# A 1024-wide mixer and attention program in float32 on one core: query, key and value products of 512 columns, a shared Nyquist row, gates behind the last pair, a later norm

## The chip, the core and the metric

The program runs on one core of one Trainium2 chip. The metric is device time in microseconds for one execution of the whole program. The profiled execution gives the span from the first to the last instruction and, for every instruction, its engine, start and duration.

## The reference, cut to what matters

512 tokens of width 1024 pass a feed-forward layer, a token mixer (short convolution, a recurrent part with eight heads of 64, two gates), a second feed-forward layer, a norm, a layer of Fourier mixing and attention ("even"), a recurrent layer ("odd") and a last norm. All is float32. The change touches the mixer's order and the even layer:

```python
def token_mixer(h, ...):
    p = h @ w_in
    pa, pb, pg = split(p)
    y_a = (b_gate * causal_dwconv(c_gate * u, conv_w)) @ w_out_a
    ...                                   # recurrent part of pb -> y
    y_b = (y * g) @ w_out_b
    g_a, g_b = split(pg)
    return (sigmoid(g_a) * y_a + sigmoid(g_b) * y_b) @ w_o

def fourier_attention_layer(x, norm_g, w_in, fourier_w, q_gain, k_gain, w_out, rope):
    h = rms_norm(x, norm_g)
    f_in, f_gate, q, k, v, a_gate = split(h @ w_in)      # 1024 1024 1024 256 256 1024
    fg = f_in.reshape(b, s, 4, 256)
    fmix = fftn(fg, axes=(1, 3), norm="ortho").real      # over tokens and 256 channels
    fmix = einsum('bsgc,gce->bsge', fmix, fourier_w)
    f_out = fmix * silu(f_gate)
    q = rope(rms_norm(q.reshape(b, s, 8, 128), q_gain))
    k = rope(rms_norm(k.reshape(b, s, 2, 128), k_gain))
    a_out = softmax(q k^T * 128 ** -0.5) v * silu(a_gate)   # four query heads to a key head
    return x + concat(f_out, a_out) @ w_out
```

## The kernel before

**Products.** Each float32 operand is split into a high part `h`, rounded to the matmul type, and a low part `l`; a product is three matmuls, h*h, h*l and l*h (`mm3`, L784). Activations lie feature-major: eight tiles of 128 features by 512 tokens, `xs` after the norm's gains. `gemm` (L790) makes 128 output features by 512 tokens: 8 k tiles x 3 = 24 matmuls of 512 columns, weights stationary. Query, key and value are wanted token-major, so `gemm_tm` (L1605) has the tokens stationary and the weights moving: for each of four token tiles 8 x 3 matmuls of 256 columns, six times over (four query groups of two heads, key, value).

**Weights.** `wload` (L739) fetches 512 KB into `raw` (three buffers), casts it into `wh` and subtracts into `wl` (four buffers each). In the first and second feed-forward layers `put_low` prepares and stores low parts of the mixer's and the odd layer's weights; `wload_low` (L756) fetches them in place of the subtraction. `group_tm` (L779) loads a group's weights in two pieces of four k tiles. Activations have 76 slots of 2 KB per partition, PSUM eight banks.

**Order.** `Rec` records every operation of the program and `schedule` (L317) plays it through with a table of costs: on each engine it issues the ready operation with the lowest `prio`, that is its place in the program plus `bias`, up to 800 places ahead of the first one not issued, as far as buffers are free. TensorE stays in its shape of matmul for some places (`choose`, L540). The order found is fixed in the program: each engine works it off in sequence. So moving a call in the program moves its priority. All instructions are recorded at one line, L555; the groups are told apart by their tiles.

**Mixer** (`_mixer`, L927). `pair(j)` prepares two heads (three products with `w_in`, chunk matrices, a small inverse through DRAM), `pair_out` (L1110) runs their recurrence in some fifty small steps and ends in `yo`, split into `ys`. `conv` and `out_a` with their gates, and the gates 34 to 41 (`gates`), are products of 24 matmuls that can lie beside these steps. `w_out_b` contracts over the four `ys`; its results, times the gates `gb` and plus `ga`, are `ms`, over which `w_o` contracts.

**Even layer** (`_even`, L1363). Two sums of squares give `rstd1` (the final norm) and `rstd` (with the layer's own norm, `rs` in the trace): adds on VectorE for the first, on GpSimd for the second, a sum over partitions by TensorE (`fold`, the tiles `rones`). For each of four groups of 256 channels: two products `e_f`, scaled by `rstd`; a transform over channels (`d1`); sum and difference of the token halves, `sd`; transforms over tokens (`seq`): `pc` of the first 128 columns, `pq` and `pn` of the second 128. Of `pn` only row 0, the Nyquist channel, is used. Then two gate products and the contraction with `fw`. After that `e_out0`, key and value, and for each query group `rot` (sum of squares, rotation), a factor of 1/rms, and two heads: gate product `e_ag`, transposes `to_fm`, scores, softmax, transposes of `e`, product with the values.

Of the kernel before, what the change touches and what calls it, by code (L numbers as in the profile page):

```python
# [142 lines left out]
def layout(i):  # L143
    f = lambda n: np.asarray(i[n], dtype=np.float32)
    o = {}
# [19 lines left out]
    o["e_qkv"] = _groups(np.ascontiguousarray(ei[:, 2048:3584]), 8, 256).reshape(6, 128, 2, 4, 256)  # L165
# [482 lines left out]
class Net:  # L648
# [130 lines left out]
    def group_tm(self, g):  # L779

        return [self.wload(self.a["e_qkv"][g][:, i], (128, 4, 256)) for i in range(2)]
# [145 lines left out]
    def _mixer(self):  # L927
# [84 lines left out]
        self.pair_out(*p.pop(0))  # L1012
        conv(3)
        p[3] = pair(3)
        out_a(0)
        self.pair_out(*p.pop(1))
# [4 lines left out]
        gates(0, 4)  # L1021
        self.pair_out(*p.pop(3))
        gates(4, 8)
# [339 lines left out]
    def _even(self):  # L1363
# [6 lines left out]
        xs = [self.split_scaled(x[k], g12[:, k:k + 1]) for k in range(KT)]  # L1370
        s1 = self.sumsq(adds="vector")
# [8 lines left out]
        V.tensor_tensor(rstd, rstd, rstd1, ALU.mult)  # L1380

# [30 lines left out]
        fo = []  # L1412
        for g in range(4):
# [23 lines left out]

            def seq(col, tr):
                ps = self.P((128, 2, 256))
                for e in range(2):  # L1440
                    h, l = sd[e]
                    for k in range(2):
                        self.mm3(ps[:, e], h[:, k, col], l[:, k, col], d2h[tr][e][:, k], d2l[tr][e][:, k], k == 0, k == 1)
# [7 lines left out]
            pn = seq(c2, 0)  # L1451
            V.tensor_copy(Q[0:1], pn[0:1])
# [42 lines left out]
        def tables(q):  # L1495
# [3 lines left out]
            for tp in range(2):  # L1499
                t = self.T(shape=(128, 2, 2, 128), p="rope")  # L1500
                for h in range(2):
                    G.tensor_tensor(t[:, :, h], rp[1][:, 2 * tp:2 * tp + 2],
                                    sw[:, q].unsqueeze(1).to_broadcast([128, 2, 128]), ALU.mult)
                s.append(t)
            return c, s

        def rot(g, tab):


            w = self.group_tm(g)  # L1510
            ms = self.sm(8)
            out = []
            for tp in range(2):
                ps = self.P((128, 2, 2, 128))
                for tt in range(2):
                    self.gemm_tm(ps[:, tt].rearrange("p h i -> p (h i)"), w, xs, 2 * tp + tt)
                s = self.T(shape=(128, 4, 128))
                A.activation(s, ps.rearrange("p t h i -> p (t h) i"), AF.Square)
                V.tensor_reduce(ms[:, 4 * tp:4 * tp + 4], s, axis=AX.X, op=ALU.add)
                t2 = self.T(shape=(128, 2, 2, 128))  # L1520
# [331 lines left out]
```

## Time and profile before

| | |
|---|---|
| median of 3 runs | 1857.87 us (1857.47 to 1860.03) |
| profiled execution | 1858.05 us, span 1856.3 us, mean granted clock 0.997 |
| TensorE, its weight loads | busy 1835.8 us (99%), 1540.4 us (83%) |
| VectorE, ScalarE, GpSimd | 1266.8 (68%), 854.5 (46%), 230.5 us (12%) |
| DMA | 341.10 MB, mean 184 GB/s |

A matmul's shown duration (0.39 us for 512 columns) is longer than the step from one to the next, because they are pipelined; the pace is read from starts or from a count over a stretch. TensorE's busy share therefore says where it waits, not how fast it is. The granted clock is in tenths of 2.4 GHz; 0.5 is its other level, 1.2 GHz. By the timeline the first feed-forward layer lies at 8 to 390 us, the mixer to about 780, the second feed-forward layer to 1140, the even layer to 1537, the odd layer to the end.

### The profile page before, as it was taken

What the parts mean: (1) busy time and instruction counts of PE and PEld (TensorE: products, weight loads), DVE (VectorE), ACT (ScalarE), POOL (GpSimd) and SP (SyncE); (2) the same over time, 40 slices, a digit from 0 to 9 for tenths busy, and PEclk for the clock granted to TensorE, in tenths of its full rate; (3) what the DMA queues carried; (4) which work ended last, traced back from release to release, by engine and by line L of the source; (5) the groups of instructions that cost most, each with busy time, mean ns of one, the idle gap of its engine ahead of it and who ended that gap; (6) DMA issues with size and microseconds to landing.
All of it is one profiled execution on the core that took longest, in us unless ns stands there. A gap on an engine that the chain in (4) does not pass through costs nothing.

```text
span 1856.3 us, 26407 instructions
## 1 busy us (share of the span) xinstructions
PE 1835.8 (99%) x10344; PEld 1540.4 (83%) x10344; DVE 1266.8 (68%) x1966; ACT 854.5 (46%) x1188; POOL 230.5 (12%) x182
## 2 busy tenths in 40 slices
PE   9999999999999999999999999999999999999997
PEld 7888888888888886888878887888999888888887
DVE  7766775579767424476567668854478966899773
ACT  6333433465243332344344246422255645897771
POOL 0100101223202003211011015110000010000002
PEclk9999999999999999999999999999999999999999
DMA  7898895436534344578888874222212125466543
GB/s 270 285 311 283 299 318 173 142 128 172 189 120 139 131 154 157 176 260 291 271 273 306 283 239 146 81 69 79 89 50 72 54 102 188 169 204 210 193 170 103
DMA packets 120398, 341.10 MB, mean 184 GB/s; under 512 B 33873, under 2 KB 36177, under 8 KB 120273
## 3 DMA queue, kind: packets, MB, share of 16 engines
q1 hardware_dynamic: 120272, 339.41, 54.6%
q8 instruction: 81, 1.33, 0.3%
q14 instruction: 45, 0.36, 0.1%
HBM read 277.76 MB, written 61.60 MB: 183 GB/s over the span
## 4 chain that ended last, share of the span: by engine, by line
PE 53%; DMA 6%; DVE 5%; ACT 1%; issue 1%; POOL 1%; SPq 0%; POOLq 0%; DVEq 0%; ACTq 0%
PE pm L555 51%; DMA raw<-o_in 3%; PE pw L555 2%; DVE wl L555 2%; DMA low<-wl 2%; ACT wh L555 1%; DMA raw<-ffn_d 1%; DVE t L555 0%; DVE l L555 0%; DMA wl<-low 0%; POOL acc L555 0%; DVE x L555 0%; DVE xl L555 0%; DVE acc L555 0%; DVE s L555 0%
## 5 line engine op out<-in xcount | busy, mean ns | idle before, releaser
L555 ACT CAST wh<-raw 128x1024 fp32r<-128x1024 f32 (+1 forms) x331 | 343.8, 1042 | 670.6 <-PE pm L555 285.2
L555 PE MATMUL pm<-xh,wl 128*128 128x512 f32 x1488 | 580.6, 390 | 1.3 <-DVE wl L555 1.1
L555 PE MATMUL pm<-xh,wh 128*128 128x512 f32 x1488 | 581.3, 391 | 0.3 <-ACT wh L555 0.3
L555 PE MATMUL pm<-xl,wh 128*128 128x512 f32 x1488 | 580.6, 390 | 0.9 <-DVE xl L555 0.9
L555 DVE TENSOR_TENSOR wl<-raw,wh 128x1024 fp32r<-128x1024 f32 (+1 forms) x302 | 383.1, 1271 | 194.9 <-DMA low<-wl 86.7
L555 PEld LDWEIGHTS pm<-xh,wl 128*128 128x128 f32 x1488 | 279.4, 188 | 60.9 <-DVE wl L555 3.9
L555 PEld LDWEIGHTS pm<-xh,wh 128*128 128x128 f32 x1488 | 279.4, 188 | 58.7 <-ACT wh L555 0.7
L555 PEld LDWEIGHTS pm<-xl,wh 128*128 128x128 f32 x1488 | 279.4, 188 | 58.6 <-DVE xl L555 1.3
L555 PE MATMUL pm<-h,wl 128*128 128x512 f32 (+1 forms) x832 | 317.8, 382 | 2.1 <-DMA wl<-low 2.1
L555 PE MATMUL pm<-h,wh 128*128 128x512 f32 (+1 forms) x832 | 316.8, 383 | 1.8 <-DVE yo L555 0.9
L555 PE MATMUL pm<-l,wh 128*128 128x512 f32 (+1 forms) x832 | 317.5, 382 | 0.0
L555 POOL TENSOR_TENSOR t<-t,t 128x512 f32<-128x512 f32 x60 | 90.3, 1507 | 915.3 <-DVE t L555 693.7
L555 PEld LDWEIGHTS pm<-h,wl 128*128 128x128 f32 x832 | 156.8, 189 | 32.3 <-DMA wl<-low 2.6
L555 PEld LDWEIGHTS pm<-h,wh 128*128 128x128 f32 x832 | 156.8, 189 | 32.4 <-DVE h L555 1.3
L555 PEld LDWEIGHTS pm<-l,wh 128*128 128x128 f32 x832 | 156.9, 189 | 30.1 <-DVE l L555 0.2
L555 DVE TENSOR_TENSOR t<-pm,rstd 128x512 f32<-128x512 f32 x146 | 98.8, 684 | 15.4 <-PE pm L555 15.3
L555 ACT ACT_TABLE_LOAD x72 | 92.4, 1283 | 17.2 <-DVE s L555 15.5
L555 DVE CAST wh<-raw 128x1024 fp32r<-128x1024 f32 x77 | 56.6, 735 | 63.9 <-PE pm L555 38.8
L555 DVE TENSOR_TENSOR x<-x,pm 128x512 f32<-128x512 f32 (+1 forms) x44 | 27.8, 637 | 68.7 <-PE pm L555 68.6
L555 ACT ACTIVATE t<-t 128x512 f32<-128x512 f32 x100 | 59.4, 625 | 26.7 <-DVE t L555 25.7
L555 POOL TENSOR_TENSOR acc<-acc,sq 128x512 f32<-128x512 f32 x28 | 46.7, 1667 | 151.1 <-ACT sq L555 151.1
L555 DVE TENSOR_TENSOR l<-t,h 128x512 fp32r<-128x512 f32 x87 | 59.7, 695 | 6.8 <-ACT h L555 5.7
(257 smaller groups left out, 2052.9 us busy)
## 6 DMA issues: line engine op xcount, KB each, us to landing
low<-wl SPq DMA_DIRECT2D x106, 512.0 KB, 3.7
wl<-low SPq DMA_DIRECT2D x106, 512.0 KB, 3.5
raw<-w_in SPq DMA_DIRECT2D x76, 512.0 KB, 4.7
raw<-o_in SPq DMA_DIRECT2D x64, 512.0 KB, 4.6
raw<-ffn_g SPq DMA_DIRECT2D x44, 512.0 KB, 4.2
raw<-ffn_u SPq DMA_DIRECT2D x44, 512.0 KB, 4.9
raw<-ffn_d SPq DMA_DIRECT2D x32, 512.0 KB, 4.9
raw<-o_out SPq DMA_DIRECT2D x32, 512.0 KB, 4.7
```

The source lines that it names most:

```text
L555: o.ins = getattr(getattr(self.nc, o.eng), o.fn)(*o.args, **o.kw)
```

## The change

Four things change. (1) The query, key and value weights are laid out as three groups of 512 columns (heads 0 to 3, heads 4 to 7, key with value), each loaded in four pieces of two k tiles; `gemm_tm` makes 512 columns for each token tile. `rot` works on one token tile, `factor` makes 1/rms for a whole group, and the loop runs over two groups of four heads. (2) Column 128 of every group's `sd` is copied into column 32 g of one zeroed tile pair `nyq`; one transform of it gives all four Nyquist rows in `pn`, so the Fourier part runs all four first halves, then this transform, then four second halves. (3) In the mixer `pair(3)` comes before `conv(3)`, the second pair's `pair_out` before `out_a(0)`, and all eight gates come behind the last `pair_out`. (4) The even layer's two sums of squares and factors are recorded with a `bias` of 100.

```diff
--- before.py
+++ after.py
@@ -162,7 +162,7 @@
     o["w_o"] = _groups(f("w_o")[0], 8, 128)
     ei = f("even_w_in_2")[0]
     o["e_f"] = _groups(np.ascontiguousarray(ei[:, 0:2048]), 8, 128)
-    o["e_qkv"] = _groups(np.ascontiguousarray(ei[:, 2048:3584]), 8, 256).reshape(6, 128, 2, 4, 256)
+    o["e_qkv"] = _groups(np.ascontiguousarray(ei[:, 2048:3584]), 8, 512).reshape(3, 128, 4, 2, 512)
     o["e_ag"] = _groups(np.ascontiguousarray(ei[:, 3584:4608]), 8, 128)
     fw = f("fourier_w_2")[0]
     lowr = fw[:, 0:128]
@@ -778,7 +778,7 @@
     def group_tm(self, g):
-        return [self.wload(self.a["e_qkv"][g][:, i], (128, 4, 256)) for i in range(2)]
+        return [self.wload(self.a["e_qkv"][g][:, i], (128, 2, 512)) for i in range(4)]
     def mm3(self, out, wh, wl, xh, xl, start, stop):
@@ -1010,17 +1010,16 @@
         conv(1)
         conv(2)
         self.pair_out(*p.pop(0))
+        p[3] = pair(3)
         conv(3)
-        p[3] = pair(3)
+        self.pair_out(*p.pop(1))
         out_a(0)
-        self.pair_out(*p.pop(1))
         out_a(1)
         out_a(2)
         self.pair_out(*p.pop(2))
         out_a(3)
-        gates(0, 4)
         self.pair_out(*p.pop(3))
-        gates(4, 8)
+        gates(0, 8)
         ms = []
         for h in range(4):
             w = self.group("w_out_b", h)
@@ -1368,6 +1367,8 @@
         o1, o2 = _VOFF["final_norm"], _VOFF["even_norm_2"]
         V.tensor_tensor(g12, self.vec[:, o1:o1 + 8], self.vec[:, o2:o2 + 8], ALU.mult)
         xs = [self.split_scaled(x[k], g12[:, k:k + 1]) for k in range(KT)]
+        self.rec.bias = 100
         s1 = self.sumsq(adds="vector")
         rstd1 = self.T(p="rs1")
         self.rsqrt(rstd1, s1, 1.0 / D, 1e-6)
@@ -1378,6 +1379,7 @@
         V.tensor_tensor(v2, v2, s2, ALU.mult)
         self.rsqrt(rstd, v2, 1.0 / D, 1e-6)
         V.tensor_tensor(rstd, rstd, rstd1, ALU.mult)
+        self.rec.bias = 0
         pt = self.W((128, 4, 128))
         for t in range(4):
@@ -1409,7 +1411,12 @@
             V.tensor_copy(p[0:1], fwr[0:1, 0, gs])
             V.tensor_copy(m[0:1], fwr[0:1, 1, gs])
             fw.append((p, m))
-        fo = []
+        nyq = [self.T(F32R, (128, 2, 2, 128), "ny") for _ in range(2)]
+        for t in nyq:
+            G.memset(t.bitcast(F32), 0.0)
+        sds = []
         for g in range(4):
             fs = []
             for m in range(2):
@@ -1434,11 +1441,22 @@
             V.tensor_tensor(s, pp[0], b, ALU.add)
             V.tensor_tensor(d, pp[0], b, ALU.subtract)
             sd = (self.split(s, (128, 2, 256)), self.split(d, (128, 2, 256)))
+            for e in range(2):
+                for t, hl in zip(nyq, sd[e]):
+                    nc.copy(t[:, e, :, 32 * g:32 * g + 1], hl[:, :, 128:129])
+            sds.append(sd)
+        ps = self.P((128, 2, 256))
+        for e in range(2):
+            for k in range(2):
+                self.mm3(ps[:, e], nyq[0][:, e, k], nyq[1][:, e, k], d2h[0][e][:, k], d2l[0][e][:, k], k == 0, k == 1)
+        pn = self.T(shape=(128, 2, 256), p="pn")
+        A.copy(pn, ps)
+        fo = []
+        for g in range(4):
             def seq(col, tr):
                 ps = self.P((128, 2, 256))
                 for e in range(2):
-                    h, l = sd[e]
+                    h, l = sds[g][e]
                     for k in range(2):
                         self.mm3(ps[:, e], h[:, k, col], l[:, k, col], d2h[tr][e][:, k], d2l[tr][e][:, k], k == 0, k == 1)
                 return ps
@@ -1448,8 +1466,7 @@
             pq = seq(c2, 1)
             Q = self.T(shape=(128, 2, 256))
             A.copy(Q, pq)
-            pn = seq(c2, 0)
-            V.tensor_copy(Q[0:1], pn[0:1])
+            V.tensor_copy(Q[0:1], pn[32 * g:32 * g + 1])
             Qs = self.split(Q, (128, 2, 256))
             fl = lambda t: t.rearrange("p e j -> p (e j)")
             if g % 2 == 0:
@@ -1492,78 +1509,87 @@
             nc.sync.dma_start(out=r, in_=self.a["rope"][:, i])
             rp.append(r)
-        def tables(q):
+        def tables(q, n):
             c = self.T(shape=(128, 4, 128), p="rope")
             G.tensor_tensor(c, rp[0], qkg[:, q].unsqueeze(1).to_broadcast([128, 4, 128]), ALU.mult)
             s = []
...
+            for t in range(4):
+                if t % (4 // n) == 0:
+                    r = self.T(shape=(128, 4, 128), p="rope")
+                o = n * (t % (4 // n))
+                G.tensor_tensor(r[:, o:o + n], rp[1][:, t:t + 1].to_broadcast([128, n, 128]),
+                                sw[:, q].unsqueeze(1).to_broadcast([128, n, 128]), ALU.mult)
+                s.append(r[:, o:o + n])
             return c, s
-        def rot(g, tab):
...
+        def rot(ps, t, n, tab, ms):
+            s = self.T(shape=(128, 4, 128))[:, 0:n]
+            A.activation(s, ps, AF.Square)
+            V.tensor_reduce(ms, s, axis=AX.X, op=ALU.add)
+            t2 = self.T(shape=(128, 4, 128))[:, 0:n]
+            half = lambda z: z.rearrange("p h (a b i) -> p (h a) b i", a=2, b=2)
+            V.tensor_tensor(half(t2), half(ps)[:, :, ::-1, :], half(tab[1][t]), ALU.mult)
+            V.tensor_tensor(s, ps, tab[0][:, t:t + 1].to_broadcast([128, n, 128]), ALU.mult)
+            G.tensor_tensor(s, s, t2, ALU.add)
+            return s
+        def factor(ms, n):
+            w = 4 * n
+            c = self.sm(16)[:, 0:w]
+            r, r2 = (z.rearrange("p (t h) -> p t h", h=2)[:, :, 0:1].to_broadcast([128, 4, n]) for z in (rt, rt2))
+            f = lambda z: z.rearrange("p (t h) -> p t h", t=4)
+            V.tensor_tensor(f(ms), f(ms), r2, ALU.mult)
             V.tensor_scalar(ms, ms, 1.0 / 128, 1e-6, op0=ALU.mult, op1=ALU.add)
...
-            V.tensor_tensor(c, c, rt, ALU.mult)
-            return out, c
+            V.tensor_tensor(f(c), f(c), r, ALU.mult)
+            return c
         def to_fm(tiles, h):
             ps = self.W((128, 4, 128))
             for t in range(4):
-                PE.transpose(ps[:, t], tiles[t // 2][:, 2 * (t % 2) + h], self.ident)
+                PE.transpose(ps[:, t], tiles[t][:, h], self.ident)
             return self.split(ps.rearrange("p t i -> p (t i)"))
...
+        w = self.group_tm(2)
+        ktab = tables(1, 2)
+        ms = self.sm(16)[:, 0:8]
+        kt, vT = [], []
+        for t in range(4):
+            ps = self.P((128, 4, 128))
+            self.gemm_tm(ps.rearrange("p h i -> p (h i)"), w, xs, t)
+            kt.append(rot(ps[:, 0:2], t, 2, ktab, ms[:, 2 * t:2 * t + 2]))
+            if t % 2 == 0:
+                vt = self.T(shape=(128, 2, 256))
+            V.tensor_scalar(vt[:, t % 2], ps[:, 2:4].rearrange("p h i -> p (h i)"), rt[:, 2 * t:2 * t + 1], None, op0=ALU.mult)
+            if t % 2:
+                vT.append(self.split(vt, (128, 2, 256)))
+        ck = factor(ms, 2)
+        for t in range(4):
+            V.tensor_tensor(kt[t], kt[t], ck[:, 2 * t:2 * t + 2].unsqueeze(2).to_broadcast([128, 2, 128]), ALU.mult)
         kF = [to_fm(kt, h) for h in range(2)]
...
-        qtab = tables(0)
+        qtab = tables(0, 4)
         at = []
-        for g in range(4):
-            qt, cq = rot(g, qtab)
+        for g in range(2):
+            w = self.group_tm(g)
+            ms = self.sm(16)
+            qt = []
+            for t in range(4):
+                ps = self.P((128, 4, 128))
+                self.gemm_tm(ps.rearrange("p h i -> p (h i)"), w, xs, t)
+                qt.append(rot(ps, t, 4, qtab, ms[:, 4 * t:4 * t + 4]))
+            cq = factor(ms, 4)
             V.tensor_scalar(cq, cq, 128.0 ** -0.5, None, op0=ALU.mult)
-            for hh in range(2):
-                h = 2 * g + hh
+            for hh in range(4):
+                h = 4 * g + hh
...
                         mx = self.sm(2, tag="mx")
                         V.tensor_reduce(mx[:, 0:1], sc, axis=AX.X, op=ALU.max)
-                        cc = cq[:, 2 * t + hh:2 * t + hh + 1]
+                        cc = cq[:, 4 * t + hh:4 * t + hh + 1]
                         V.tensor_scalar(mx[:, 0:1], mx[:, 0:1], cc, -1.0, op0=ALU.mult, op1=ALU.mult)
                         e = self.T(shape=(128, 4, 128), p="e")
                         A.activation(e.rearrange("p a i -> p (a i)"), sc, AF.Exp, bias=mx[:, 0:1], scale=cc,
@@ -1607,8 +1633,8 @@
         sl = slice(t * 128, t * 128 + 128)
         n = len(xs)
         for k, (xh, xl) in enumerate(xs):
-            h, l = w[k // 4]
-            self.mm3(out, xh[:, sl], xl[:, sl], h[:, k % 4], l[:, k % 4], k == 0, k == n - 1)
+            h, l = w[k // 2]
+            self.mm3(out, xh[:, sl], xl[:, sl], h[:, k % 2], l[:, k % 2], k == 0, k == n - 1)
     def odd(self):
```

## Rows read from the trace of the kernel before

**Rows 1.** The page, parts 1 and 2: busy time by engine; granted clock in 40 slices.

```profile
PE 1835.8 (99%) x10344; PEld 1540.4 (83%) x10344; DVE 1266.8 (68%) x1966; ACT 854.5 (46%) x1188; POOL 230.5 (12%) x182
...
PEclk9999999999999999999999999999999999999999
```

**Rows 2.** The chain of waits, a long run of 512-column products (start us, us, what).

```profile
955.21 162.35 PE pm L555 x715
```

**Rows 3.** The timeline of TensorE in the key product (start us, us, what).

```profile
1320.00 0.28 PE L555 MATMUL pm<-wh,xh 128*128 128x256 f32 x1
...
1321.20 0.28 PE L555 MATMUL pm<-wl,xh 128*128 128x256 f32 x1
```

**Rows 4.** Groups by form, whole span: busy us, mean ns of one, idle before.

```profile
L555 ACT CAST wh<-raw 128x1024 fp32r<-128x1024 f32 x315 | 330.3, 1052 | 637.4 <-PE pm L555 259.7 <-DMA raw<-ffn_u 74.1 <-DMA raw<-w_in 66.7
...
L555 PE MATMUL pm<-wh,xh 128*128 128x256 f32 x192 | 55.3, 288 | 0.0
```

**Rows 5.** Windows, us; TensorE, its loads, VectorE, ScalarE, GpSimd busy (count); clock, DMA, GB/s.

```profile
721.00:740.00 19.00, 15.09 (x59) 11.42 (x58) 13.55 (x17) 7.94 (x11) 14.65 (x10) 0.91 0.59 214
735.90:739.30 3.40, 3.40 (x8) 2.72 (x9) 3.05 (x3) 2.08 (x4) 3.40 (x3) 0.51 1.02 413
1140.00:1172.00 32.00, 28.83 (x124) 22.61 (x123) 27.79 (x30) 16.03 (x21) 9.48 (x3) 1.00 0.45 143
1172.00:1318.00 146.00, 146.00 (x768) 125.88 (x767) 86.11 (x123) 41.22 (x54) 10.44 (x10) 1.00 0.23 75
1395.10:1433.20 38.10, 38.10 (x257) 35.00 (x256) 32.28 (x74) 23.70 (x40) 2.56 (x3) 1.00 0.17 57
1433.20:1471.50 38.30, 38.30 (x257) 35.05 (x256) 35.39 (x92) 21.96 (x37) 2.59 (x3) 1.00 0.16 55
1471.50:1500.00 28.50, 28.08 (x161) 24.02 (x160) 24.62 (x68) 17.23 (x30) 0.16 (x1) 1.00 0.13 46
```

**Rows 6.** The chain of waits from 700 to 760 us.

```profile
721.41 0.82 DVE yo L555
...
728.88 6.96 DMA wl<-low
```

**Rows 7.** The timeline: one row of ScalarE, two of TensorE, one of VectorE.

```profile
671.09 0.58 ACT L555 COPY vT<-pw 128x512 f32<-128x512 f32 x1
...
1146.23 0.50 PE L555 MATMUL pm<-xl,wh 128*128 128x512 f32 x1 [0.91 <-DVE xl L555]
...
1150.41 0.50 PE L555 MATMUL pm<-h,rones 128*128 128x512 f32 x1 [2.19 <-ACT h L555]
...
1171.35 0.69 DVE L555 TENSOR_TENSOR rs<-rs,rs 128x512 f32<-128x512 f32 x1
```

**Rows 8.** The tile acc, 1110 to 1155 us: shortest/median/longest ns, first and last start.

```profile
L555 POOL TENSOR_TENSOR acc<-acc,sq x7: 1282/1742/5378, 1118.3 to 1144.3; 128x512 f32<-128x512 f32 x7
```

**Rows 9.** Groups by form from 670 to 721 us.

```profile
L555 PE MATMUL pm<-xh,wl 128*128 128x512 f32 x33 | 13.1, 397 | 0.0
...
L555 PE MATMUL pm<-h,wl 128*128 128x512 f32 x21 | 8.3, 395 | 0.0
```

**Rows 10.** Groups by form of VectorE from 1395.1 to 1433.2 us.

```profile
L555 DVE TENSOR_TENSOR wl<-raw,wh 128x1024 fp32r<-128x1024 f32 x4 | 4.9, 1216 | 0.6 <-ACT wh L555 0.6
...
L555 DVE TENSOR_TENSOR t<-pm,rope 128x512 f32<-128x512 f32 x4 | 2.8, 689 | 0.1
```

**Rows 11.** Groups by form from 1172 to 1318 us.

```profile
L555 ACT COPY t<-pm 128x512 f32<-128x512 f32 x8 | 4.7, 588 | 10.9 <-PE pm L555 10.8
...
L555 DVE COPY rt<-pw 128x8 f32<-128x8 f32 x1 | 0.2, 158 | 0.0
```

**Rows 12.** DMA issues, 1300 to 1500 us: count, KB each, median us to landing.

```profile
raw<-e_qkv SPq DMA_DIRECT2D x9, 512.0 KB, 3.6
```

**Rows 13.** The timeline of TensorE: last wide product, first narrow one behind it.

```profile
701.51 0.39 PE L555 MATMUL pm<-xl,wh 128*128 128x512 f32 x1
701.83 0.27 PE L555 MATMUL pw<-zb,MN 64*64 64x64 f32 x2
```

More of the change, by code (lines that the diff above doesn't have):

```diff
@@ L1498, in tables @@
             s = []
[L1499 to L1504, printed above, removed]
-            return c, s
-        def rot(g, tab):
[L1510 to L1520, printed above, removed]
-                V.tensor_tensor(t2.rearrange("p t h (a b i) -> p (t h a) b i", a=2, b=2),
-                                ps.rearrange("p t h (a b i) -> p (t h a) b i", a=2, b=2)[:, :, ::-1, :],
-                                tab[1][tp].rearrange("p t h (a b i) -> p (t h a) b i", a=2, b=2), ALU.mult)
-                V.tensor_tensor(s.rearrange("p (t h) i -> p t h i", t=2), ps,
-                                tab[0][:, 2 * tp:2 * tp + 2].unsqueeze(2).to_broadcast([128, 2, 2, 128]), ALU.mult)
-                G.tensor_tensor(s, s, t2.rearrange("p t h i -> p (t h) i"), ALU.add)
-                out.append(s)
-            c = self.sm(8)
-            V.tensor_tensor(ms, ms, rt2, ALU.mult)
@@ L1532, in rot @@
             V.reciprocal(c, c)
-            t = self.sm(8)
+            t = self.sm(16)[:, 0:w]
             V.tensor_tensor(t, c, c, ALU.mult)
@@ L1543, in to_fm @@
             for t in range(4):
-                PE.transpose(ps[:, t], tiles[t // 2][:, 2 * (t % 2) + h], self.ident)
+                PE.transpose(ps[:, t], tiles[t][:, h], self.ident)
             return self.split(ps.rearrange("p t i -> p (t i)"))
-        kt, ck = rot(4, tables(1))
-        for tp in range(2):
-            V.tensor_tensor(kt[tp], kt[tp], ck[:, 4 * tp:4 * tp + 4].unsqueeze(2).to_broadcast([128, 4, 128]), ALU.mult)
-        kF = [to_fm(kt, h) for h in range(2)]
-        w = self.group_tm(5)
@@ L1552, in _even @@
-        vT = []
-        for tp in range(2):
-            ps = self.P((128, 2, 256))
-            for tt in range(2):
-                self.gemm_tm(ps[:, tt], w, xs, 2 * tp + tt)
-            t = self.T(shape=(128, 2, 256))
-            V.tensor_tensor(t, ps, rt.rearrange("p (t h) -> p t h", h=2)[:, 2 * tp:2 * tp + 2, 0:1].to_broadcast([128, 2, 256]), ALU.mult)
-            vT.append(self.split(t, (128, 2, 256)))
-        qtab = tables(0)
-        at = []
-        for g in range(4):
-            qt, cq = rot(g, qtab)
+        w = self.group_tm(2)
```

## The prediction

> **What bounds the kernel now.** The page comes first: TensorE is busy 99% of the 1856.3 us span, its clock is at its upper level in every slice [rows 1]. So a gain must come from fewer or cheaper matmuls, or from the few places where TensorE waits or its clock falls. The pace is next. In a stretch without a wait, 715 matmuls take 162.35 us, 0.227 us for one of 512 columns [rows 2]; ten steps of 256 columns take 1.20 us, 0.120 us each [rows 3]. Two of 256 therefore cost 0.240 us against 0.227 for one of 512. The groups by form give the count for query, key and value: 192 of each of three kinds [rows 4]. The windows and TensorE's own waits give the places. From 721 to 740 us TensorE is idle 19.00 - 15.09 = 3.91 us [rows 5], behind the last pair's `yo` and a low part of `w_o`'s weights that takes 6.96 us to land [rows 6]. From 1140 to 1172 us 124 matmuls take 32.00 us where 124 x 0.227 = 28.15 would do: 3.85 us too long [rows 5]; the waits are for `xl` and for the sum of squares [rows 7].
>
> **The change part by part.** The sum is made against the profiled execution: span 1856.3 us, 1858.05 us with what lies around it, 0.18 us above the median.
>
> *Query, key and value.* 576 products of 256 columns become 288 of 512: 576 x 0.120 = 69.1 against 288 x 0.227 = 65.4 us. TensorE sets the pace there, so 3.7 us come off the path. Loads, splits of weights and elements read from PSUM stay; three factor chains in place of five and some narrower vector instructions are hidden beside TensorE. Two things may eat the gain. The weights of a group now fill all four `wh` and `wl` buffers; I cost this at nothing, because the first pair of k tiles is free once all four token tiles have used it, and a new one needs 1.05 us of cast and 1.22 us of subtraction [rows 4, 10], while the 18 products that follow on the last token tile take 4.1 us. The other is the order: the query products came in four blocks of 11.5 us between the heads and now come in two of 21.8. A cycle of two heads takes 38.10 us of TensorE and 32.28 of VectorE [rows 5]. Of the latter some 8.0 belong to the query block (two subtractions, four rotations at 0.69 [rows 10], reductions and factor, estimated from these), so a head without query products is 13.3 us on TensorE and 12.1 on VectorE, 91%. VectorE was at 35.39 of 38.30 and, without query products, 24.62 of 28.50 us in the last two stretches [rows 5]. At the first share the last four heads lose nothing; at the second they take 48.4 / 0.864 = 56.0 in place of 53.2 us. So this part is worth 0.9 to 4.1 us (3.7 and the 0.42 us of idle time in 1471.5 to 1500 [rows 5]); I take 3.7, since the first is the busier row.
>
> What is left beside the columns is 2 x 0.120 - 0.227 = 0.013 us a matmul [rows 2, 3]. [...]
>
> *Nyquist row.* Per group the third transform of the second stage (2 x 2 x 3 = 12 products) goes; one run of 12 does all four groups. 36 products fewer, 36 x 0.120 = 4.3 us. Added are two clears on GpSimd, 16 copies of one column (the copy of eight columns takes 0.16 us [rows 11]), one evacuation, and the last group's spectrum must be there before the first group's second half. VectorE is busy 86 of 146 us there [rows 5], and the first transforms of four groups, with products of the next group ready, cover each other. Without that cover it is one chain, once: an evacuation of 0.59 us [rows 11] and a row's copy, taken as long. I take 4.3, bounds 3.1 and 4.3.
>
> *Mixer.* The same products in another order of priority. The window says why TensorE ran dry: from 670 to 721 us, beside the last pair's chain, it did 98 products of gates (33 of two kinds, 32 of the third) and 63 of `w_out_b` (21 of each kind) [rows 9]; these ran out, and all that remained of `w_out_b` needed the last pair's result. Its weights still filled the buffers, so those of `w_o` came in one burst, one of them in 6.96 us [rows 6]. Behind it the clock was at 0.51 (1.2 GHz, the lower level) for 3.4 us, in which eight matmuls were started [rows 5], each 0.2 us longer: 1.6 us. With 3.91 idle this is 5.5 us. With the gates behind the last pair, its chain starts some four gates (4 x 24 x 0.227 = 21.8 us) earlier, and eight gates and three quarters of `w_out_b`, 43.6 + 16.3 = 59.9 us, lie beside a chain that took some 50 (its transposed values are copied at 671.09, `yo` begins at 721.41 [rows 6, 7]): `yo` should be there before the cover ends, and `w_o`'s weights come at the normal rate. What is late next is the sum of the last output column (multiply, GpSimd add, split), under 21 ready products of 4.8 us. I take 5.0, bounds 3.5 and 5.5. The fourth pair's start before the last convolution, and the second pair's end before the first `out_a`, only move cover from one chain to another. A change between wide and narrow products costs about 0.1 us (a step of 0.32 in place of 0.227 [rows 13]); some 20 such changes more or fewer make 2 us either way, taken as nothing.
>
> *Even layer's norm.* Its squares, adds and folds now stand 100 places later in priority. VectorE's seven adds no longer come ahead of `xl` and of the second weights; the folds, which stopped TensorE while GpSimd's last add took 5.38 us [rows 8], fall behind one or two more groups of `e_f`. The factor was ready at 1172 [rows 7]. If it slips by two groups (10.9 us) to 1183, `e_f` still has room: eight PSUM banks at 24 x 0.227 = 5.45 us each last from 1140 to 1183.6. Of 3.85 us I take 3.2; the low bound is 1.8 (the `xl` wait of 0.91 and half of the 2.19 us [rows 7] stay).
>
> Sum: 3.7 + 4.3 + 5.0 + 3.2 = 16.2 us, 1858.05 - 16.2 = 1841.9. With all low bounds, 0.9 + 3.1 + 3.5 + 1.8 = 9.3 us less, 1848.8; with all high ones and 2 us of fewer changes, 19.7 less, 1838.3.
>
> **The rivals.** *The mixer's stall only moves (0.13).* The order is a planner's priority, so gates may still be used up early, or an earlier pair runs dry. For it: it ran dry behind 161 products that stood there as cover [rows 9]. Against: four gates more behind the chain. Then 16.2 - 5.0 = 11.2 us, 1847; with 2 us of new waits, 1849.
>
> *The norm comes too late (0.08).* GpSimd's adds stretch from 1.28 to 5.38 us beside VectorE [rows 8]. If that goes on, the factor slips by more than 11 us, the eight banks are full and TensorE waits, which I price at three quarters of one product's 5.45 us: 4 us lost for 3.2 gained, 1858.05 - 16.2 + 7.2 = 1849. Against: the next 100 places hold about two groups. The Trainium skill (SBUF — State Buffer, section Who interferes with whom) has the shared port of VectorE and GpSimd as an exclusive lock; by that rule, which agrees with the long add, moving the adds beside other VectorE work does not shorten them.
>
> *VectorE sets the pace of attention (0.08).* If both groups of four heads run at 13.3 x 56.0 / 53.2, 5.6 us go: 1847 or 1848; with a dry start of each group (4 us for rotation, transposes and split, some six instructions of 0.6 to 0.7 us [rows 10, 11]), up to 1856.
>
> *A wide product costs twice a narrow one (0.02).* If 512 columns in the token-major form take 2 x 0.120 us, query, key and value give nothing: 1841.9 + 3.7 = 1845.6. The 0.227 of the other products of 512 columns [rows 2] speaks against it. [...]
>
> *Slower: the four weight buffers (0.05).* If a group of four tiles keeps every buffer to its end, and its fourth tile can be fetched only when a raw buffer is free, each of the three groups waits 3.6 us for the landing [rows 12], 1.05 for the cast and 1.22 for the subtraction, and behind each wait the clock is low as at 736 us (1.6 us): 3 x 7.5 = 22.5, 1841.9 + 22.5 = 1864.4. From 16.2 / 3 = 5.4 us a group on it is slower than before. Against: a load is a pair of k tiles, and with two pairs loaded TensorE can go on with all four token tiles.
>
> **How the numbers follow.** The forecast has 0.64, 1841.9 us, its own range 1838 to 1849. To hold 8 in 10 the range is 1836 to 1850: it takes in the first, second and fourth rival, most of the third, and 2 us below the sum for waits that go with the ones removed. About 0.2% (3.7 us) is what a measurement here can tell from no change. Faster by more: 0.64 + 0.13 + 0.06 + 0.04 + 0.02 = 0.89; within it 0.07 (the bad ends of the second and third rival and the mild ones of the last); slower 0.04.
>
> **What would show it.** Right: 288 products of 512 columns at 0.227 us in the token-major form, 36 fewer of the 256-column ones; no drop of the clock at the mixer's end, TensorE's waits for `yo` and `wl<-low` gone; the fold's wait gone and the first evacuation with `rs` not before 1172 us on the same scale. Wrong: a wait for `wl` or `wh` at a query group, VectorE above 92% in the last heads with TensorE idle over 2 us, a wait for a PSUM bank at the even layer's start, or a new gap between pairs in the mixer.

## The result, and the profile after

The changed kernel takes 1845.7 us, the median of four runs (1843.86 to 1846.5), against 1857.67 (1855.56 to 1860.03) for the kernel before on the same chip: ratio 0.9936, interval 0.9921 to 0.9951, so 11.9 us less, between 9.1 and 14.7. The forecast was 1841.9 with a range of 1836 to 1850: the side and the range hold, the sum of 16.2 us does not. The profiled execution of after is the fastest of its four, 1843.86 us with a span of 1842.1, and lies 14.2 us under the profiled one of before; part of the work below is to say which of the two figures is the change.

The page of after, part 1 (as [rows 1]):

```profile
PE 1825.8 (99%) x10020; PEld 1518.6 (82%) x10020; DVE 1273.7 (69%) x1961; ACT 855.3 (46%) x1197; POOL 235.1 (13%) x189
```

There are 324 matmuls fewer, as the diff says: 288 by the wider products and 36 by the shared row. TensorE is still the bound. What it waits for, in after (us in total, times, longest):

```profile
...
PE pm L555 <- ACT h L555: 1.3, 1, 1.3
PE pm L555 <- ACT ny L555: 1.0, 1, 1.0
...
PE pm L555 <- DVE xl L555: 0.6, 1, 0.6
PE pm L555 <- DVE ny L555: 0.5, 1, 0.5
PE pw L555 <- DVE yc L555: 0.5, 1, 0.5
PE pw L555 <- DVE zb L555: 0.4, 1, 0.4
...
```

Three more, of 1.6, 1.3 and 0.6 us, stand at the two ends of the kernel and in before as well. `yo` and `wl<-low` [rows 6] are gone. The wait for `xl` [rows 7] is shorter but there; a fold still waits for `h`, but it is the fold of the other sum (see the norm below). `ny` is new: it is the tile that collects the Nyquist column. The last two lie between the pairs of the mixer, with two more of 0.3 and 0.2 us; before has only one of 0.2 us (`yc`) there. The windows of after (columns as in [rows 5]), one for each place:

```profile
390.00:680.00 290.00, 288.58 (x2878) 239.06 (x2877) 203.19 (x458) 124.15 (x203) 62.07 (x58) 1.00 0.46 144
680.00:745.00 65.00, 65.00 (x308) 52.69 (x308) 26.75 (x51) 20.76 (x25) 16.36 (x11) 1.00 0.64 214
900.00:1030.00 130.00, 130.00 (x575) 107.54 (x574) 81.02 (x88) 50.97 (x54) 13.08 (x10) 1.00 0.84 280
1135.00:1172.00 37.00, 35.13 (x178) 29.17 (x177) 36.04 (x45) 18.91 (x28) 2.87 (x2) 1.00 0.34 113
1190.00:1215.00 25.00, 23.47 (x134) 19.72 (x133) 18.15 (x24) 8.72 (x15) 9.40 (x7) 1.00 0.18 53
1425.00:1450.00 25.00, 24.81 (x133) 20.84 (x132) 23.87 (x59) 17.48 (x27) 1.66 (x2) 1.00 0.39 127
```

The same stretches of before, where [rows 5] has none that answers:

```profile
390.00:680.00 290.00, 289.59 (x2730) 239.18 (x2729) 196.56 (x447) 125.47 (x198) 56.84 (x55) 1.00 0.47 148
...
900.00:1030.00 130.00, 128.91 (x568) 106.09 (x567) 82.73 (x89) 52.28 (x55) 11.14 (x8) 1.00 0.83 282
...
1135.00:1172.00 37.00, 33.83 (x146) 26.75 (x145) 32.78 (x36) 20.73 (x29) 14.45 (x5) 1.00 0.43 138
...
1190.00:1215.00 25.00, 25.00 (x133) 21.60 (x132) 17.81 (x27) 6.78 (x10) 9.72 (x10) 1.00 0.13 43
```

Span minus busy time of TensorE gives the idle time. The mixer's end has none left, but the pairs ahead of it, 390 to 680 us, lose 1.42 us in place of 0.41. The feed-forward at 900 to 1030 us, which nothing in the diff touches, lost 1.09 us in before and loses none in after. The start of the even layer loses 1.87 in place of 3.17. The spectral part, 1190 to 1215, loses 1.53 where before lost nothing.

The token-major products of after run at the pace that was expected, here thirteen steps from one product of 512 columns to the next in 2.94 us, 0.226 each:

```profile
1342.70 0.39 PE L555 MATMUL pm<-wh,xh 128*128 128x512 f32 x1
...
1345.64 0.39 PE L555 MATMUL pm<-wl,xh 128*128 128x512 f32 x1
```

And this is the new loss, on TensorE (in brackets the idle time ahead and what ended it):

```profile
1197.57 0.28 PE L555 MATMUL pm<-h,ny 128*128 128x256 f32 x1
...
1199.62 0.47 PE L555 MATMUL pm<-h,ny 128*128 128x256 f32 x2 [0.95 <-ACT ny L555]
...
1201.07 0.50 PE L555 MATMUL pm<-h,ny 128*128 128x256 f32 x2 [0.51 <-DVE ny L555]
...
1201.64 0.40 PE L555 MATMUL pm<-xh,wl 128*128 128x512 f32 x1
```

From 1197.57 to 1201.64 us the twelve products of the Nyquist row and three of 512 columns are done. At 0.120 and 0.227 us [rows 2, 3] they want 2.12 us and take 4.07: 1.95 lost. In after VectorE is then doing this, the last split of the fourth group and its column (timeline):

```profile
1197.47 2.38 DVE L555 TENSOR_TENSOR l<-t,h 128x512 fp32r<-128x512 f32 x2
1199.88 1.13 DVE L555 CAST ny<-l 128x2 fp32r<-128x2 f32 x1
```

and GpSimd this, the rotation tables of the attention that comes 110 us later:

```profile
1195.96 2.73 POOL L555 TENSOR_TENSOR rope<-t,qkgs 128x512 f32<-128x512 f32 x2
1199.32 1.67 POOL L555 TENSOR_TENSOR rope<-t,qkgs 128x512 f32<-128x512 f32 x1 [0.63 <-DVE l L555]
```

A copy of two columns takes 1.13 us; it ends at 1201.01 us, with GpSimd's product (1200.99). In the prediction the tables have no line at all.

With these rows the 14.2 us between the two profiles come out as 3.7 (pace of query, key and value) + 4.3 (36 products) + 5.5 (mixer's end: 3.91 idle and 1.6 of low clock) + 1.3 (even layer's start) + 1.1 (feed-forward) - 1.95 (`ny`) - 1.0 (pairs of the mixer) = 12.95; 1.2 us stay unexplained. Of the two figures the 11.9 us are the change: the profiled execution of after lies 1.8 us under its median and that of before 0.4 us above, and this alone is 2.2 of the 14.2 us.

### The profile page after: what moved, and what is told of

The parts are those of the page before. It is cut to its first block, busy times and chain, and to the rows that moved or that the text cites. A ratio compares the mean times of both kernels' runs of the same rounds, so it can differ in the third digit from the quotient of the medians.

```text
span 1842.1 us, 25754 instructions
## 1 busy us (share of the span) xinstructions
PE 1825.8 (99%) x10020; PEld 1518.6 (82%) x10020; DVE 1273.7 (69%) x1961; ACT 855.3 (46%) x1197; POOL 235.1 (13%) x189
## 4 chain that ended last, share of the span: by engine, by line
PE 87%; DMA 5%; DVE 5%; ACT 2%; issue 1%; SPq 0%; POOL 0%; POOLq 0%; ACTq 0%; DVEq 0%
PE pm L555 83%; PE pw L555 4%; DMA raw<-w_in 2%; DVE wl L555 2%; DMA raw<-ffn_d 1%; ACT wh L555 1%; DMA raw<-ffn_u 1%; DVE t L555 1%; DVE l L555 0%; DMA raw<-e_f 0%; ACT xh L555 0%; DVE wh L555 0%; SPq L555 0%; ACT sq L555 0%; DVE u L555 0%
## 5 line engine op out<-in xcount | busy, mean ns | idle before, releaser
L555 ACT CAST wh<-raw 128x1024 fp32r<-128x1024 f32 (+1 forms) x337 | 350.7, 1042 | 673.5 <-PE pm L555 269.8
L555 POOL TENSOR_TENSOR t<-t,t 128x512 f32<-128x512 f32 (+1 forms) x63 | 91.3, 1450 | 864.3 <-DVE t L555 783.1
L555 DVE CAST wh<-raw 128x1024 fp32r<-128x1024 f32 x71 | 50.2, 707 | 51.0 <-PE pm L555 23.9
L555 POOL TENSOR_TENSOR acc<-acc,sq 128x512 f32<-128x512 f32 x28 | 42.5, 1516 | 180.8 <-ACT sq L555 180.6
```

The source lines that it names most:

```text
L555: o.ins = getattr(getattr(self.nc, o.eng), o.fn)(*o.args, **o.kw)
```

## The experiments

Four questions: what is each part worth alone, where does the new loss in the spectral part come from, why did the norm give so little, and which edit of the mixer does the work. Ratios are to the kernel before, run beside each kernel; 0.001 is 1.86 us.

### Each part alone

Query, key and value alone; in the diff of this part only these lines and the rotation code behind them:

```diff
-    o["e_qkv"] = _groups(np.ascontiguousarray(ei[:, 2048:3584]), 8, 256).reshape(6, 128, 2, 4, 256)
+    o["e_qkv"] = _groups(np.ascontiguousarray(ei[:, 2048:3584]), 8, 512).reshape(3, 128, 4, 2, 512)
...
-        qtab = tables(0)
+        qtab = tables(0, 4)
```

> The kernel before with the query, key and value products of 512 columns alone. Theory (the gain is the pace, 576 x 0.120 against 288 x 0.227 us): 3.7 us less, 1854.0. Rival 1 (VectorE sets the pace of the last heads, or a group start runs dry): 0.9 us less or nothing, 1856.9 to 1857.7, with more idle time of TensorE in the last heads. Rival 2 (the parts help each other, so alone this part loses what the early start of the layer hides): under 2 us less, with waits for weights at the query groups. Both rivals would leave the shortfall of the whole change, 12 us measured against a sum of 16.2, with this part.

Ratio 0.9989 (0.998 to 0.9998): 2.0 us less, 0.4 to 3.7. The profile has no more idle time in attention; the loss is elsewhere, with a wait of 1.17 us for `l` at 1202. TensorE and VectorE of this kernel there:

```profile
1202.11 0.50 PE L555 MATMUL pm<-l,h 128*128 128x512 f32 x1 [1.17 <-DVE l L555]
```

```profile
1198.88 1.50 DVE L555 CAST h<-t 128x512 fp32r<-128x512 f32 x1
1200.42 1.64 DVE L555 TENSOR_TENSOR l<-t,h 128x512 fp32r<-128x512 f32 x1
```

and GpSimd beside it, the query's table, now four products of 512 columns where before had four of 256:

```profile
1198.82 6.62 POOL L555 TENSOR_TENSOR rope<-t,qkgs 128x512 f32<-128x512 f32 x4
```

So neither rival as written: by the trace part of the gain is lost, but 100 us ahead of the products that it belongs to. In before the same table has half the columns and comes later, at 1208.59 us and on, so its size and its place have both changed.

The Nyquist row alone, part (2) of the change; of its diff only the last lines:

```diff
-            V.tensor_copy(Q[0:1], pn[0:1])
+            V.tensor_copy(Q[0:1], pn[32 * g:32 * g + 1])
```

> The kernel before with the shared Nyquist row alone. Sum of the prediction: 36 products of 0.120 us less, 4.3 us, 1853.4. Theory from the trace of the changed kernel, where TensorE waits 1.5 us for the tile ny and loses about as much again between narrow and wide products: 4.3 - 2.5 = 1.8 us less, 1855.9, with a wait for ny on TensorE. Rival: the wait for ny belongs to the earlier start of the layer in the whole change and not to this part; then 4.3 us less and no wait for ny.

Ratio 0.9972 (0.9962 to 0.9982): 5.2 us less, 3.3 to 7.1. TensorE has no wait for `ny` here: no table product runs when the copy of two columns starts, and it takes 0.17 us. The rival holds: the part is worth its 4.3 us, and the wait for `ny` comes when it stands beside the other parts.

The mixer's order alone, and its gates alone; the diff is that of the gates, the whole order moves the pairs as well:

```diff
-        gates(0, 4)
         self.pair_out(*p.pop(3))
-        gates(4, 8)
+        gates(0, 8)
```

> The kernel before with the mixer's order alone. Prediction: 5.0 us less, 1852.7 (3.9 idle and 1.6 of low clock go, 0.5 come back). Theory from the trace of the changed kernel: 5.5 us, and 1.7 more because the feed-forward behind it is planned afresh and its wait for low weights at 920 to 960 us goes too: 7.2 us less, 1850.5. Rival (that wait goes by another part, or comes back): 5.0 to 5.5 with the wait for wl still there at about 920 to 960 us.

> The kernel before with the eight gates behind the last pair_out, the order of pairs and convolutions as it was. Theory (the gain at the mixer's end is cover: four gates more, 21.8 us of products beside the last chain): no idle time from 715 to 745 us, as with the mixer's whole order, 3.8 us less or more, ratio 0.998 or under. Rival (the last pair's earlier start is what brings the end earlier): the wait for yo or for low weights is still there, shorter, and under 2 us are gained.

The whole order gives 0.998 (0.997 to 0.999), 3.7 us less, against 5.0 in the prediction and 7.2 in this run's own theory; the gates alone 0.9974 (0.9965 to 0.9984), 4.8 us less. The last window of the kernel with the gates alone, to set beside [rows 5]:

```profile
715.00:745.00 30.00, 30.00 (x134) 24.84 (x133) 14.47 (x23) 8.28 (x10) 12.01 (x8) 1.00 0.76 268
```

No idle time, no low clock: the cover theory holds, and moving pairs and convolutions adds no gain that can be measured. It has a cost that the traces show: TensorE's waits for `aT`, `t` and `zb`, 0.2, 0.3 and 0.4 us between 500 and 600 us, stand in all eight profiles of kernels with the pairs moved and in none of the six others. The gates alone beside the other three parts were not run. The waits of the feed-forward expected to go with it did not (129.64 and 129.16 us busy of 130 at 900 to 1030): they come and go between executions, see the last section.

The norm's priority alone:

```diff
+        self.rec.bias = 100
         s1 = self.sumsq(adds="vector")
...
+        self.rec.bias = 0
```

> The kernel before with the later priority of the even layer's norm alone. Prediction: 3.2 us less, 1854.5. Theory from the trace of the changed kernel, where the fold's wait and that for xl shrink but stay (2.7 us lost there in place of 4.3): 1.6 us less, 1856.1. Rival (the fold's remaining wait comes from the other parts' plan, not from this one): 3 us less and no wait for h at the fold.

Ratio 0.9989 (0.998 to 0.9998): 2.0 us less, 0.4 to 3.7. Two waits are still there in its timeline at the places of [rows 7], for `xl` and at a fold:

```profile
1144.76 0.50 PE L555 MATMUL pm<-xl,wh 128*128 128x512 f32 x1 [0.58 <-DVE xl L555]
...
1148.63 0.50 PE L555 MATMUL pm<-h,rones 128*128 128x512 f32 x1 [1.07 <-ACT h L555]
```

The four parts give 2.0 + 5.2 + 3.7 + 2.0 = 12.9 us, the whole change 11.9: they add up within the intervals. But each figure is uncertain by some 1.7 to 1.9 us either way, too much to tell whether the parts disturb each other; the traces show one place where they do, the wait for `ny`, which no part has alone.

### The rotation tables

The tables are tied to a tile that is ready late, so that GpSimd can't make them beside the spectral part:

```diff
+        qk0, qkg = qkg, self.T(shape=(128, 2, 128), p="qkg")
+        V.scalar_tensor_tensor(qkg.rearrange("p q i -> p (q i)"), fo[7][0][:, 0:256], 0.0,
+                               qk0.rearrange("p q i -> p (q i)"), op0=ALU.mult, op1=ALU.add)
```

> The changed kernel with the rotation tables on GpSimd held back until e_f's last output tile is there (one VectorE instruction on 256 columns ties them to it, adding zero times that tile). Theory (VectorE's subtractions and the ny copy of 1.13 us run long beside GpSimd's table products, and so TensorE waits 1.5 us for ny and loses 2.6 us in 1180 to 1220): nearly all of it comes back, 2 to 2.6 us less than the changed kernel, ratio 0.992, subtractions of 0.69 us there. Rival (it is the Nyquist row's own chain, evacuation and copy, once): the wait for ny stays, ratio 0.9936. Second rival (the tables cost as much where they go, beside e_out): a new loss of 1 to 2 us at 1250 to 1300.

Ratio 0.9921 (0.9907 to 0.9934): 1842.53 us, its four runs (1842.1 to 1843.09) all under the four of the changed kernel, which were measured in another set. Window of this kernel:

```profile
1190.00:1215.00 25.00, 25.00 (x151) 22.37 (x150) 16.12 (x25) 10.34 (x16) 0.00 (x0) 1.00 0.21 76
```

VectorE's groups from 1185 to 1212 us, in after and then here (busy us, mean ns):

```profile
L555 DVE TENSOR_TENSOR l<-t,h 128x512 fp32r<-128x512 f32 x6 | 5.7, 956 | 0.1
...
L555 DVE CAST ny<-l 128x2 fp32r<-128x2 f32 x1 | 1.1, 1134 | 0.0
```

```profile
L555 DVE TENSOR_TENSOR l<-t,h 128x512 fp32r<-128x512 f32 x8 | 5.3, 686 | 0.1
...
L555 DVE CAST ny<-l 128x2 fp32r<-128x2 f32 x1 | 0.2, 169 | 0.0
```

With nothing on GpSimd the subtraction takes 686 ns in place of 956 and the copy 169 in place of 1134; the wait for `ny` is gone. Where the tables are made now, 1264 to 1276 us beside `e_out`, TensorE loses nothing: VectorE has little to do there. The first theory holds, both rivals fall.

The same in the kernel before with query, key and value alone:

```diff
...
+        V.scalar_tensor_tensor(qkg.rearrange("p q i -> p (q i)"), fo[7][0][:, 0:256], 0.0,
+                               qk0.rearrange("p q i -> p (q i)"), op0=ALU.mult, op1=ALU.add)
```

> The kernel before with the query, key and value part alone and the rotation tables held back until e_f's last output tile is there, as in the run that held them back in the changed kernel. Theory (the part's 3.7 us fell to about 1.8 because the query table on GpSimd grew from four products of 256 columns to four of 512, and VectorE's subtraction and cast beside it took 1.64 and 1.50 us with TensorE waiting 1.2 us): 3.5 us less than before, 1853.8, ratio 0.9981 or under, and no wait of TensorE at 1195 to 1215. Rival (the missing 1.9 us are lost in attention itself, VectorE setting the pace): as with the part alone, 1855.5, ratio 0.999.

Ratio 0.9982 (0.9973 to 0.9991), 3.3 us less in place of 2.0; the wait at 1202 is gone (25.00 of 25.00 us busy from 1190 to 1215). The trace decides for the theory; the two ratios alone, whose intervals overlap, would not.

### The norm

Twice the delay in priority:

```diff
-        self.rec.bias = 100
+        self.rec.bias = 200
```

> The changed kernel with a bias of 200 in place of 100 for the even layer's norm. In the order of issue 100 puts the first fold 33 products behind the start of e_f, 7 more than before; 200 puts it behind 77, that is the one or two groups that the prediction counted on, and VectorE's last xl ahead of the last adds. Theory (the norm gave 1.9 us in place of 3.2 because the fold hardly moved): the waits for the fold's h and for xl go, 1.3 to 2.5 us less than the changed kernel, ratio to the kernel before 0.992 to 0.993 in place of 0.9936. Rival (too late: the factor's chain takes 17 us and the transposes now stand 74 products, 16.8 us, behind the fold): a wait of 1 to 4 us for rs at the transposes takes the place of the two, ratio 0.9936 to 0.995.

> The changed kernel with both: bias 200 and the tables held back. If the two losses are separate: 3.5 to 5 us less than the changed kernel, 1841 to 1842, ratio 0.9910 to 0.9918. If one hides the other: no better than the better of the two alone.

Ratio 0.9916 (0.9902 to 0.9929), a little under the theory's 0.992 to 0.993, but not for its reason. The first fold now stands behind 77 products and waits for nothing; TensorE waits ahead of it instead, for the last `xh` and `xl`:

```profile
1140.70 0.51 PE L555 MATMUL pm<-xh,wh 128*128 128x512 f32 x1 [0.69 <-ACT xh L555]
1142.21 0.50 PE L555 MATMUL pm<-xl,wh 128*128 128x512 f32 x1 [1.00 <-DVE xl L555]
1154.82 0.39 PE L555 MATMUL pm<-h,rones 128*128 128x512 f32 x1
```

```profile
1135.00:1172.00 37.00, 35.31 (x155) 28.68 (x154) 29.18 (x29) 16.67 (x22) 4.65 (x3) 1.00 0.36 127
```

Idle there 1.69 us against 1.87 in after: nothing won. What this kernel did win, by its trace, is in the spectral part, 0.20 us idle from 1190 to 1215 in place of 1.53, where VectorE came later to the small tile `qkgs` that the sine tables need, and GpSimd made them only from 1207 us. The idle times make up 1.5 us, the ratios 3.7, in intervals that overlap. The run with both edits agrees: 0.992 (0.9907 to 0.9934), no better than the tables alone, so the later fold adds nothing of its own that can be measured.

Then what holds the last `xh`? ScalarE's timeline in that same kernel (bias 200):

```profile
1136.28 1.05 ACT L555 CAST wh<-raw 128x1024 fp32r<-128x1024 f32 x1 [1.49 <-DMA raw<-e_f]
1137.24 0.72 ACT L555 ACTIVATE xh<-x,g 128x512 fp32r<-128x512 f32 x1
```

ScalarE stood still for 1.49 us in front of a cast of `e_f`'s weights that had not landed, with `xh` queued behind; VectorE's next `xl` then waited 1.01 us for that `xh`. In SP's queue, here in the timeline of after, the loads of the second transform's matrix (`dft2`) and of `fw` stand ahead of `e_f`'s:

```profile
1109.48 4.45 SPq L555 DMA_DIRECT2D raw<-dft  x2
1115.83 3.69 SPq L555 DMA_DIRECT2D raw<-fw  x2
1121.94 11.97 SPq L555 DMA_DIRECT2D raw<-e_f  x5
```

`e_f` begins at 1132 us; the matrix is first used at about 1190, by the first group's `pc`, and `fw` behind it. The next two kernels move these two blocks (on top of the tables held back):

```diff
-        fw = []
-        for gp in range(2):
...
+        fw = []
+        for gp in range(2):
+            fwr = self.wt((128, 2, 2, 256), F32, "raw")
...
         fo = []
```

> The changed kernel with the tables held back and the block that loads fw and makes its sums and differences (two loads of 512 KB, four GpSimd sums, four one-row copies on VectorE) moved from ahead of e_f to behind the Nyquist row. Theory (what is left of the norm's stall, 2.2 to 2.7 us of lost time in 1130 to 1160 whether the fold stands behind 33 or 77 products, comes from work queued ahead of the last xh and xl: casts of e_f's weights on ScalarE that wait for loads behind fw's, and VectorE's copies beside GpSimd): the waits for xl and h go, 1.5 to 2.5 us less than with the tables alone, ratio 0.9908 to 0.9913. Rival (the stall is the chain of the last x itself, evacuation, cast, subtraction): the same 2.3 us lost, ratio 0.992.

Ratio 0.9907 (0.9893 to 0.992). The waits for `xl` and `h` are gone; one of 0.96 us for the factor `rs` takes their place:

```profile
1166.71 0.66 PE L555 MATMUL pw<-cst,rs 128*128 128x128 f32 x4 [0.96 <-DVE rs L555]
```

```profile
1135.00:1172.00 37.00, 36.04 (x171) 29.98 (x170) 33.19 (x41) 16.17 (x22) 11.57 (x6) 1.00 0.34 114
```

ScalarE's `xh` casts now wait for VectorE's `x` and no longer for weights. The block holds loads, four sums on GpSimd and four copies on VectorE; which of these did the most was not taken apart.

```diff
-        d2h, d2l = [], []
-        for tr in range(2):
...
+        d2h, d2l = [], []
+        for tr in range(2):
...
         ps = self.P((128, 2, 256))
```

> As the run before it, and the two loads of the second transform's matrix with their eight casts and subtractions also behind the first transforms. Theory: e_f's first weights are the first in the queue, so the last of the stall goes, 0 to 1 us less than the run before it, ratio 0.990 to 0.991. Rival (too late: the splits of the matrix now stand on VectorE and ScalarE ahead of the second transforms): a new wait of 1 to 4 us at 1180 to 1230, ratio 0.991 to 0.993.

Ratio 0.9902 (0.9888 to 0.9915), 1839.83 us (1839.67 to 1840.21), the lowest median of the study and 18.2 us under the kernel before:

```profile
1135.00:1172.00 37.00, 36.93 (x175) 30.70 (x174) 32.64 (x41) 13.49 (x20) 7.42 (x5) 1.00 0.34 114
```

0.07 us of idle time is left at the layer's start, and no wait over 0.2 us from 1100 to 1345. The times can't tell this kernel from the one before it, the idle time does. The last kernel takes the norm's priority back to where it was:

```diff
-        self.rec.bias = 100
+        self.rec.bias = 0
```

> The run with fw's block and the second transform's matrix moved back, but with a bias of 0 for the norm: the fold again stands at the place in priority that it had in the kernel before, here 20 products behind the start of e_f instead of 44. Theory (priority of the norm matters where the fold's inputs are later than the fold's place: here GpSimd's adds of the second sum end after the first group): a wait of 1.5 to 4 us for h at the fold comes back, ratio 0.991 to 0.9925 against 0.9902. Rival (what delayed the fold was only the work that has been moved away, and the later priority is worth nothing any more): no wait over 0.3 us there, ratio 0.9902.

Ratio 0.9918 (0.9904 to 0.9933), 1842.14 us (1841.34 to 1843.78). Its window and its two waits:

```profile
1135.00:1172.00 37.00, 35.91 (x173) 29.06 (x172) 33.03 (x40) 15.97 (x23) 7.42 (x5) 1.00 0.29 100
```

```profile
1138.16 0.50 PE L555 MATMUL pm<-h,rones 128*128 128x512 f32 x1 [0.39 <-DVE h L555]
...
1166.06 0.39 PE L555 MATMUL pm<-h,h 128*128 128x256 f32 x1 [0.61 <-ACT h L555]
```

Between the two theories: the fold waits, but 0.39 us and not 1.5 to 4; the other 0.61 us are a wait of the first transform. By the profile the later priority is worth 1.0 us here (1.09 idle against 0.07); by the times 3 us, in intervals that overlap. That it is worth something is likely; how much stays open.

## Why the prediction was right, and where its sum was wrong

*Query, key and value: 3.7 taken.* The pace was right (0.226 us), and so was the cover: VectorE is at 23.87 of 25 us in the last group of heads, 95%, and TensorE is idle for 0.19. The rivals of the weight buffers, of VectorE's pace and of the wide product at twice a narrow one fall. The last is nearly what the Trainium skill (TensorE: Matmul & The Clock Gate, section Back-to-back issue gap) gives for an isolated warm matmul, N/2.4 ns and a fixed 2.5 ns; for a stream of weight loads and matmuls the section says that this does not hold. The trace, such a stream, has 0.227 us at 512 columns and 0.120 at 256. The step that failed is the sentence that the rest is "hidden beside TensorE": it lists loads, splits, chains and vector instructions, and leaves out `tables(0, 4)`, whose sine table doubles. That work is done early, beside VectorE's splits in the spectral part. Alone the part gave 2.0 us, with the tables held back 3.3; the intervals overlap, and the wait of 1.17 us that is gone decides.

*Nyquist row: 4.3 taken.* Right by itself (5.2, 3.3 to 7.1). In the whole change 1.95 us of it went into the wait for `ny`. The prediction had that chain, priced at an evacuation and a row's copy and taken as covered. The chain waited elsewhere: at the last split and at a copy of two columns, both stretched by the tables on GpSimd. The Trainium skill (SBUF — State Buffer, section Who interferes with whom) calls the port that VectorE and GpSimd share an exclusive lock. The trace agrees: the copy takes 1134 ns with the tables, ending with GpSimd's product, and 169 without. The prediction used that rule for the norm's adds, where it looked for trouble, and not for the tables, which it had not listed.

*Mixer: 5.0 taken.* The mechanism was right at the mixer's end: no idle time from 680 to 745 us. The rival (the stall only moves) holds in small: the moved pairs "only move cover from one chain to another" by the prediction, taken at nothing, and the three waits that came with them are 0.9 us, the "new gap between pairs" that it named as a sign of being wrong. The size was off: 3.7 us (1.9 to 5.6) for the order, 4.8 (3.0 to 6.5) for the gates alone. The 5.5 us of [rows 5] were one execution. Five profiles of kernels with the mixer as before, over 715 to 745 us, have 3.91, 3.26, 3.55, 3.88 and 3.77 us idle, and in two of the five the clock did not fall, so that the 1.6 us were never there. Before and the kernel with query, key and value alone:

```profile
715.00:745.00 30.00, 26.09 (x106) 20.25 (x106) 19.46 (x32) 10.68 (x15) 14.81 (x10) 0.94 0.55 200
```

```profile
715.00:745.00 30.00, 26.74 (x118) 20.98 (x116) 20.24 (x32) 11.12 (x16) 14.85 (x10) 1.00 0.55 198
```

*Norm: 3.2 taken, low bound 1.8.* It gave 2.0 alone, and 1.3 us of idle time in the whole change. The failed step is "fall behind one or two more groups of `e_f`" (24 or 48 products), said of both folds. The fold of GpSimd's sum, which waited 2.19 us in before, went back by 21 products, from behind 27 of `e_f` to behind 48, and waits no more. The fold of VectorE's sum went back by 7, from behind 26 to behind 33, and TensorE now comes to it before VectorE's last add has ended, at 1141.50, and been split. After, on TensorE and VectorE:

```profile
1142.20 0.50 PE L555 MATMUL pm<-h,rones 128*128 128x512 f32 x1 [1.28 <-ACT h L555]
...
1146.19 0.39 PE L555 MATMUL pm<-h,rones 128*128 128x512 f32 x1
```

```profile
1140.82 0.68 DVE L555 TENSOR_TENSOR acc<-acc,sq 128x512 f32<-128x512 f32 x1
```

A bias of 100 counts recorded operations, and between the norm and `e_f` these are for the most part the norm's own and those that prepare the matrices. The run that did put both folds two groups further back shows that the step behind it failed too: the stall did not end with the folds. It went to the next late thing, the last `xh` and `xl`, held by work queued ahead of them: weights behind loads that nobody wanted yet, and what is done with those loads. Nor did the factor slip: `rs` was at 1162 us in after, which starts the layer 7.7 us earlier; that is 1170 on the scale of before, where the prediction had "not before 1172", an error that cost nothing.

The wait at the fold was also priced without a clock behind it. In three of the six profiles with the norm as before (Nyquist row alone, mixer's order alone, gates alone) the granted clock fell to the lower level behind that wait, and in before it did not. With the Nyquist row alone, 6 products started in 2 us where before has 11:

```profile
1152.00:1154.00 2.00, 2.00 (x6) 1.62 (x5) 2.00 (x3) 1.97 (x3) 0.00 (x0) 0.50 0.19 47
```

*What was not in the sum:* 1.1 us of the feed-forward, which comes and goes between executions.

So the measured time fell into the range through margins put there for other things, the low bound of the norm and the rival of the moved stall, and not through anything said of the tables. That is luck as far as the tables go.

## What to carry to other kernels

List what a change does to every engine and every queue, tables and constants too, and look up where the planner will do them, which may be far ahead of their use. Before pricing a stall at its full length, ask which input would be the next late one, and delay that in thought: a wait ends at the last of them. A loss read from one execution is an upper or a lower end: look at the same place in a second one before it becomes a term of a sum.

## What was not expected of the hardware

A copy of 128x2 elements on VectorE took 1134 ns beside table products on GpSimd and 169 ns without; subtractions 956 against 686. An instruction that has almost no data can be as long as the other engine's.

The kernel's scatter of some 5 us (27 runs of before in one set: 1855.07 to 1860.06) shows in the traces as idle time at places that depend on transfers: 1.09 us at 900 to 1030 us in one profile of before, behind subtractions that waited for stores of low parts, none in the kernels that changed only the Nyquist row or the norm, whose code is the same up to there, and 3.26 to 3.91 at the mixer's end, with or without a fall of the clock to 1.2 GHz behind it.
